# Input norm of an encoder block: scale and shift moved behind the transposes, and a new order of the first steps

## The chip, the cores and the metric

The kernel runs on one core of one Trainium2 chip. The metric is the device time of one execution in microseconds. Times of before are a median of three runs and one profiled execution of the same program.

## The reference, cut to what matters

The block has 512 tokens of 1024 features (D). What the change touches is the first norm and the first projection:

```python
mu = mean(x); var = mean((x - mu)**2)
u = (x - mu) * rsqrt(var + 1e-5) * ln_in_g + ln_in_b      # per token, g and b per feature
q, k, v, cb, cc, ch, ga, gb = split(u @ w_in)             # w_in: 1024 columns each for q, k, v and so on
mix = ...                                                 # attention, short convolution, gates
x = layer_norm(ALPHA * u + mix) ; x = layer_norm(ALPHA * x + moe(x))
```

So `u` is needed twice: transposed (features on partitions) as the operand of the projection, and as it is, by token, for the residual sum much later.

## The kernel before

Tokens lie in four tiles `u(0)` to `u(3)` of 128 rows, two to a page (`u_68`, `u_69` in the lists below). Every product with a weight is made of three float32r products: the activations are split into a high part (`uth`) and the rest (`utl`), and a weight unit of 256 columns into `hi_in` and `lo_in`. `Unit.split` makes these parts in two halves of four of the eight feature chunks each: ScalarE (ACT) casts `raw_in` to `hi_in`, and VectorE (DVE) or GpSimd (POOL) subtracts.

The order of the work is written out by hand: each engine takes its instructions in the order in which the Python code issues them. All loads named here go through SyncE's (SP's) queue, in code order too.

The start of the kernel has these steps:

- `bias_tile(h)`, four times: two products of TensorE (PE) and two copies by ACT, for the attention's relative bias.
- Per token tile: statistics (`norm_stats`, `norm_steps`: two BN_STATS, one BN_AGGR and a chain of nine small DVE instructions ending in `ln_rs`), then the norm. Tiles 0 and 1 take it on DVE as four instructions over 512 columns (`normalize`, L114 and L115), with `ln_in_g` and `ln_in_b` held as rows broadcast to 128 partitions (`gb_in`, 512 KB each). Tiles 2 and 3 take it in pieces on ACT, POOL and DVE (`normalize_apart`).
- `transpose_split`: eight PE transposes of a tile into two PSUM banks, then per bank one ACT cast to `uth` and one DVE subtraction to `utl`.
- `v_group(j, tt)`: 24 products of token tile tt with weight unit j (columns of v), then a DVE copy to `V`. There are 16 of them, written v00, v10, v01 and so on in this document (unit first, tile second). Three PSUM banks (`ps_mm`) hold their results.

After the sixteen v groups the projections by column follow (`col_group`, L509 to L511), and the rest of the block, which the change leaves as it is.

Pages are 22 buffers of 8 KB per partition; a load waits until the page that it takes is free.

Of the kernel before, what the change touches and what calls it, by code (L numbers as in the profile page):

```python
# [37 lines left out]
def block(ctx: ExitStack, tc, a, out, dump=None, stop=None):  # L38
# [228 lines left out]
    def transpose_split(src, dst_h, dst_l, tt):  # L267

        for i in range(2):
            ps = ps_tp.tile([128, 512], F32, name="tp")  # L270
            for k in range(4):
                nc.tensor.transpose(ps[:, k * 128:(k + 1) * 128],
                                    src[:, (i * 4 + k) * 128:(i * 4 + k + 1) * 128], ident)
            psv = ps.rearrange("p (k t) -> p k t", k=4)
            o = dst_h[i][:, :, tt * 128:(tt + 1) * 128]
            nc.scalar.copy(o, psv)
            nc.vector.tensor_sub(dst_l[i][:, :, tt * 128:(tt + 1) * 128], psv, o.bitcast(F32))
# [18 lines left out]
    def normalize_apart(t, mv, rs, g, b):  # L296

        nb = work.tile([128, 1], F32, name="ln_nb")
        nc.vector.scalar_tensor_tensor(nb, mv[:, 0:1], -1.0, rs, op0=OP.mult, op1=OP.mult)
        for h in HALF:  # L300
            nc.scalar.activation(t[:, h], t[:, h], AF.Identity, scale=rs, bias=nb)
            nc.gpsimd.tensor_mul(t[:, h], t[:, h], g[:, h])
        yield
        for h in HALF:
            nc.vector.tensor_add(t[:, h], t[:, h], b[:, h])

    moments = {}

    def input_steps(tt):
# [2 lines left out]
        moments[tt] = next(steps)
        yield
        yield from steps

    def apart(tt):
        return normalize_apart(u(tt), *moments[tt], g_in, b_in)
# [21 lines left out]
    together(input_steps(0))
    normalize(u(0), *moments[0], g_in, b_in)  # L340
    units[0].split(nc.gpsimd)
    transpose_split(u(0), UTH, UTL, 0)
# [1 line left out]
    chain = input_steps(1)
    next(chain)
    together(chain)
    normalize(u(1), *moments[1], g_in, b_in)
    units[1].split(nc.gpsimd, nc.gpsimd)
    state["split"] = 2
    v_group(0, 0)  # L350
    chain = input_steps(2)
    next(chain)
# [1 line left out]
    transpose_split(u(1), UTH, UTL, 1)
    together(chain)
    half = apart(2)
    next(half)
    together(input_steps(3))
    v_group(1, 0)
    together(half)  # L360
    half = apart(3)
    next(half)
    v_group(0, 1)
    v_group(1, 1)
    transpose_split(u(2), UTH, UTL, 2)
# [1 line left out]
    together(half)
    v_group(0, 2)
    transpose_split(u(3), UTH, UTL, 3)
    prm = setup[0:42, 1152:1280]  # L370
# [973 lines left out]
```

## Time and profile before

| | us |
|---|---|
| median of 3 runs | 1162.05 (1161.49 to 1163.46) |
| the profiled execution, its own time | 1163.4 |
| its span in the profile | 1161.7 |
| PE busy in the span | 1086.0 |
| DVE, ACT, POOL busy | 467.4, 274.9, 127.9 |

The span is cut by the first column group, whose first product starts at about 78.2 us. Everything that the change moves stands ahead of it, except the two loads of `gb_in` and the eight new DVE instructions that stand by the last v groups. The timeline is read per engine: start, duration, and in brackets how long the engine was idle before and what ended that. A row with xN holds N instructions that followed each other.

### The profile page before, as it was taken

How to read it: one execution, taken by the hardware profiler on the slowest of the kernel's cores; microseconds unless marked ns; L12 is line 12 of the kernel's file. 1: busy time of each engine (PE TensorE's matmuls, PEld its weight loads, DVE VectorE, ACT ScalarE, POOL GpSimd, SP SyncE). 2: the span in 40 equal slices, each digit the busy share in tenths (PEclk: the TensorE clock that was granted, in tenths of full speed). 3: DMA queues.
4: the chain of work that ended last, by engine and by line, in shares of the span. 5: the costliest groups of instructions: out<-in, count | busy, mean ns of one | idle time of the engine just before them, and what ended most of it. 6: DMA issues, size and time to landing. Idle time of an engine off the chain costs nothing.

```text
span 1161.7 us, 17381 instructions
## 1 busy us (share of the span) xinstructions
PE 1086.0 (93%) x7145; PEld 723.6 (62%) x7145; DVE 467.4 (40%) x1018; ACT 274.9 (24%) x491; POOL 127.9 (11%) x110
## 2 busy tenths in 40 slices
PE   5999999989999999999949998999999999999994
PEld 3998877767888888888945443545454544445442
DVE  6621565654244343147781123323223222322256
ACT  3403545743023323233221111111111111111002
POOL 2304322311000000023342000000000000000000
PEclk9999999999999999999968999999999999999997
DMA  8332212122332232434195899999999999999941
GB/s 302 106 118 72 74 37 73 52 84 82 109 103 79 73 106 75 145 113 141 40 395 199 318 409 359 411 394 410 399 408 408 395 409 401 409 407 356 409 165 74
DMA packets 103324, 264.86 MB, mean 228 GB/s; under 512 B 4528, under 2 KB 49644, under 8 KB 102732
## 3 DMA queue, kind: packets, MB, share of 16 engines
q1 hardware_dynamic: 102444, 262.53, 60.3%
q8 instruction: 59, 0.97, 0.3%
q10 hardware_dynamic: 576, 1.05, 0.2%
q0 software_dynamic: 224, 0.15, 0.2%
q14 instruction: 21, 0.17, 0.0%
HBM read 260.30 MB, written 3.41 MB: 227 GB/s over the span
## 4 chain that ended last, share of the span: by engine, by line
PE 84%; DVE 11%; DMA 1%; ACT 1%; issue 1%; POOL 1%; SPq 0%; ACTq 0%; DVEq 0%; POOLq 0%
PE gu L947 19%; PE mm L510 10%; PE mm L511 10%; PE mm L509 10%; PE y L974 10%; PE x L1005 5%; PE x L907 3%; PE x L908 3%; PE pv L460 2%; PE mm L287 2%; PE mm L289 2%; PE mm L288 2%; PE lg L434 1%; PE x L919 1%; DVE u L1007 1%
## 5 line engine op out<-in xcount | busy, mean ns | idle before, releaser
L509 PE MATMUL mm<-uth,hi_in 128*128 128x512 f32 x448 | 178.7, 399 | 0.0
L511 PE MATMUL mm<-uth,lo_in 128*128 128x512 f32 x448 | 174.5, 390 | 0.0
L510 PE MATMUL mm<-utl,hi_in 128*128 128x512 f32 x448 | 174.4, 389 | 0.0
L947 PE MATMUL gu<-wg,xg 128*32 128x512 f32 (+1 forms) x1024 | 133.4, 593 | 0.0
L947 PE MATMUL gu<-wu,xg 128*32 128x512 f32 (+1 forms) x1024 | 133.3, 592 | 0.0
L974 PE MATMUL y<-wd,ht 128*32 128x512 f32 (+1 forms) x1024 | 114.9, 601 | 0.7 <-ACT ht L966 0.7
L1007 DVE TENSOR_TENSOR u<-u,x 128x512 f32<-128x512 f32 x120 | 76.7, 684 | 52.1 <-PE x L1005 52.1
L510 PEld LDWEIGHTS mm<-utl,hi_in 128*128 128x128 f32 x448 | 84.2, 188 | 18.5 <-issue 1.0
L509 PEld LDWEIGHTS mm<-uth,hi_in 128*128 128x128 f32 x448 | 84.2, 188 | 18.4 <-issue 0.5
L511 PEld LDWEIGHTS mm<-uth,lo_in 128*128 128x128 f32 x448 | 84.1, 188 | 17.5
L957 DVE SCALAR_TENSOR_TENSOR h<-h,w,gu 128x512 f32<-128x512 f32 x16 | 12.0, 748 | 179.5 <-PE gu L947 179.5
L947 PEld LDWEIGHTS gu<-wu,xg 128*32 128x32 f32 x1024 | 33.3, 110 | 76.6 <-issue 73.0
L1005 PE MATMUL x<-ys,st 128*128 128x512 f32 x240 | 68.1, 405 | 12.5 <-DVE u L1007 7.1
L947 PEld LDWEIGHTS gu<-wg,xg 128*32 128x32 f32 x1024 | 32.9, 110 | 74.6 <-issue 70.9
L974 PEld LDWEIGHTS y<-wd,ht 128*32 128x32 f32 x1024 | 32.0, 111 | 72.4 <-issue 70.2
L169 POOL TENSOR_TENSOR lo_in<-raw_in,hi_in 128x1024 fp32r<-128x1024 f32 x25 | 59.1, 2384 | 146.3 <-ACT hi_in L168 95.7
L907 PE MATMUL x<-S,xh 128*128 128x256 f32 (+1 forms) x256 | 68.6, 301 | 0.6 <-POOL over L1030 0.6
L168 ACT CAST hi_in<-raw_in 128x1024 fp32r<-128x1024 f32 x64 | 63.6, 1045 | 14.9 <-DVE lo_wa L169 8.9
L908 PE MATMUL x<-S,xl 128*128 128x256 f32 (+1 forms) x256 | 66.1, 292 | 0.0
L169 DVE TENSOR_TENSOR lo_in<-raw_in,hi_in 128x1024 fp32r<-128x1024 f32 x39 | 46.0, 1220 | 46.1 <-ACT hi_in L168 45.9
L983 DVE TENSOR_TENSOR ys<-y,ys 128x512 fp32r<-128x512 f32 x30 | 20.6, 691 | 103.1 <-ACT ys L981 103.1
L1005 PEld LDWEIGHTS x<-ys,st 128*128 128x128 f32 x240 | 41.3, 188 | 25.0 <-DVE u L1007 13.1
(301 smaller groups left out, 1589.9 us busy)
## 6 DMA issues: line engine op xcount, KB each, us to landing
wg<-in_w_gate_e SPq DMA_DIRECT2D x64, 1024.0 KB, 12.5
wu<-in_w_up_e SPq DMA_DIRECT2D x64, 1024.0 KB, 12.9
wd<-in_w_down_e SPq DMA_DIRECT2D x64, 1024.0 KB, 9.3
raw_in<-in_w_in SPq DMA_DIRECT2D x32, 1024.0 KB, 5.6
raw_wa<-in_w_a_proj SPq DMA_DIRECT2D x4, 1024.0 KB, 5.1
raw_wb<-in_w_b_proj SPq DMA_DIRECT2D x4, 1024.0 KB, 5.1
raw_wo<-in_w_o SPq DMA_DIRECT2D x4, 1024.0 KB, 5.8
u<-in_x SPq DMA_DIRECT2D x4, 512.0 KB, 11.7
```

The costliest lines, as they stand in the source:

```text
L168: nc.scalar.copy(self.hi[:, k], self.raw[:, k])
L169: eng.tensor_sub(self.lo[:, k], self.raw[:, k], self.hi[:, k].bitcast(F32))
L287: nc.tensor.matmul(o, lh(k)[:, sl], unit.hi[:, k], start=(k == 0), stop=False)
L509: nc.tensor.matmul(ps, unit.hi[:, k, sl], xh(k), start=(k == 0), stop=False)
L510: nc.tensor.matmul(ps, unit.hi[:, k, sl], xl(k), start=False, stop=False)
L511: nc.tensor.matmul(ps, unit.lo[:, k, sl], xh(k), start=False, stop=(k == KC - 1))
L907: nc.tensor.matmul(o, part(XH, tt)[:, sl], r, start=(tt == 0), stop=False)
L908: nc.tensor.matmul(o, part(XL, tt)[:, sl], r, start=False, stop=(tt == NT - 1))
L947: nc.tensor.matmul(t[32 * p:32 * p + 32], disp[i // 2][:, k, base + 32 * p:base + 32 * p + 32], of_rows(w, sel, p), start=(k == 0), stop=( ...
L974: nc.tensor.matmul(Y[hf][32 * p:32 * p + 32], ht[:, f, 32 * p:32 * p + 32], of_rows(w, sel, p), start=(f == 0), stop=(f == 3))
L1005: nc.tensor.matmul(ps, l, r, start=(n == 0), stop=(n == len(terms) - 1))
L1007: nc.vector.tensor_add(o, o, ps)
```

## The change

The norm in front of the transposes now only subtracts the mean and multiplies by `ln_rs`. Tile 0 does it as one DVE instruction over 1024 columns (L315), tiles 1 to 3 as one ACT instruction (L319). Scale and shift come after the transposes, where a feature lies on a partition: `gcol` holds `ln_in_g` and `ln_in_b` as 16 columns (two small loads, one PE transpose, one ACT copy), and each 128-column piece of a transposed tile is copied from PSUM to a new SBUF tile `y_in` with its column of scale and shift: four pieces on DVE (first bank, L283) and four on ACT (second bank, L285). The cast to `uth` and the subtraction to `utl` then read `y_in`. The broadcast rows are loaded later, and `finish_input` applies them to `u` itself by two DVE instructions of 128x1024 per tile, behind the four groups v30 to v33.

The order of the steps changes as well; POOL no longer takes part in it. In the diff `together` runs its arguments in turns, a step each.

```diff
     nc.sync.dma_start(u(0), x_rows[0])
+    prm = setup[0:42, 1152:1280]
+    for i, n in enumerate(("ln_in_g", "ln_in_b")):
+        nc.sync.dma_start(prm[8 * i:8 * i + 8], a[n].rearrange("(k p) -> k p", p=128))
     nc.sync.dma_start(onehot, a["bucket_onehot"])
-    gb_in = page("gb_in", (128, 2, D))
-    for j, n in enumerate(("ln_in_g", "ln_in_b")):
-        nc.sync.dma_start(gb_in[:, j], a[n].rearrange("(o d) -> o d", o=1).to_broadcast([128, D]))
-    g_in, b_in = gb_in[:, 0], gb_in[:, 1]
...
-    def transpose_split(src, dst_h, dst_l, tt):
+    def turn_in(tt):
+        y = att.tile([128, KC, 128], F32, name="y_in", tag="p", bufs=3)
         for i in range(2):
             ps = ps_tp.tile([128, 512], F32, name="tp")
...
+            for j in range(4):
+                k = 4 * i + j
+                g, b, p = gcol[:, k:k + 1], gcol[:, 8 + k:9 + k], ps[:, j * 128:(j + 1) * 128]
+                if i == 0:
+                    nc.vector.tensor_scalar(y[:, k], p, g, b, op0=OP.mult, op1=OP.add)
+                else:
+                    nc.scalar.activation(y[:, k], p, AF.Identity, scale=g, bias=b)
+            o = UTH[i][:, :, tt * 128:(tt + 1) * 128]
+            part = y[:, 4 * i:4 * i + 4]
+            nc.scalar.copy(o, part)
+            nc.vector.tensor_sub(UTL[i][:, :, tt * 128:(tt + 1) * 128], part, o.bitcast(F32))
+            yield
...
+    def input_norm(tt, eng):
+        steps = norm_steps(norm_stats(u(tt)))
+        mv, rs = next(steps)
+        together(steps)
+        if eng is nc.vector:
+            nc.vector.tensor_scalar(u(tt), u(tt), mv[:, 0:1], rs, op0=OP.subtract, op1=OP.mult)
+        else:
+            nb = work.tile([128, 1], F32, name="ln_nb")
+            nc.vector.scalar_tensor_tensor(nb, mv[:, 0:1], -1.0, rs, op0=OP.mult, op1=OP.mult)
+            nc.scalar.activation(u(tt), u(tt), AF.Identity, scale=rs, bias=nb)
...
     bias_tile(0)
+    input_norm(0, nc.vector)
+    together(turn_in(0), units[0].split_steps())
+    input_norm(1, nc.scalar)
+    units[1].split()
+    v_group(0, 0)
+    together(turn_in(1))
     bias_tile(1)
+    input_norm(2, nc.scalar)
+    v_group(0, 1)
+    v_group(1, 0)
+    together(turn_in(2))
+    v_group(1, 1)
     bias_tile(2)
+    input_norm(3, nc.scalar)
+    v_group(0, 2)
+    together(turn_in(3))
+    units[2].split()
+    state["split"] = 3
     bias_tile(3)
+    v_group(2, 0)
+    gb_in = page("gb_in", (128, 2, D))
...
+    def finish_input(tt):
+        nc.vector.tensor_mul(u(tt), u(tt), gb_in[:, 0])
+        nc.vector.tensor_add(u(tt), u(tt), gb_in[:, 1])
...
-        v_group(2, tt)
+        if tt:
+            v_group(2, tt)
...
         v_group(3, tt)
+        finish_input(tt)
```

The groups on PE stood in the order v00, v10, v01, v11, v02, v12, v03, v13, v20 to v33; now they stand as v00, v01, v10, v11, v02, v20, v12, v03, v13, v21 to v33. (The loop of the third unit, which held v20, now begins with v21.)

Three places show it in the engines' own order. On DVE, from the end of tile 1's chain (`ln_rs`) on, before:

```order
L85 TENSOR_TENSOR ln_rs<-ln_i,ln_t 128x1
L114 SCALAR_TENSOR_TENSOR u_68<-u_68,ln_mv,gb_in 128x512
L115 SCALAR_TENSOR_TENSOR u_68<-u_68,ln_rs,gb_in 128x512
L114 SCALAR_TENSOR_TENSOR u_68<-u_68,ln_mv,gb_in 128x512
L115 SCALAR_TENSOR_TENSOR u_68<-u_68,ln_rs,gb_in 128x512
L294 COPY v_117<-mm 128x256
L100 BN_STATS ln_st<-u_69 128x6 x2
L107 BN_AGGR ln_mv<-ln_st 128x2
L277 TENSOR_TENSOR utl_115<-tp,uth_113 128x4x128
L277 TENSOR_TENSOR utl_116<-tp,uth_114 128x4x128
```

And the same place now (`lo_in_200` is the rest of weight unit 1, `v_116` the copy of v00):

```order
L85 TENSOR_TENSOR ln_rs<-ln_i,ln_t 128x1
L318 SCALAR_TENSOR_TENSOR ln_nb<-ln_mv,ln_rs 128x1
L168 TENSOR_TENSOR lo_in_200<-raw_in_106,hi_in_199 128x1024 x2
L307 COPY v_116<-mm 128x256
L283 TENSOR_SCALAR y_in<-tp,gcol 128x128 x4
L289 TENSOR_TENSOR utl_114<-y_in,uth_112 128x4x128
L289 TENSOR_TENSOR utl_115<-y_in,uth_113 128x4x128
L100 BN_STATS ln_st<-u_69 128x6 x2
L107 BN_AGGR ln_mv<-ln_st 128x2
```

The two subtractions of weight unit 1 came from POOL to DVE and stand between tile 1's norm and its copies. Tile 2's statistics stand behind tile 1's last subtraction, and no longer in front of both.

On ACT, the first instructions behind the copies of the first bias tile, before (`hi_in_149` is unit 0, `hi_in_197` unit 1):

```order
L168 CAST hi_in_149<-raw_in_104 128x1024 x2
L276 CAST uth_113<-tp 128x4x128
L276 CAST uth_114<-tp 128x4x128
L329 COPY bias_119<-lg 128x512
L329 COPY bias_119<-lg 128x128
L168 CAST hi_in_197<-raw_in_107 128x1024 x2
```

And now (`hi_in_161` is unit 0, `hi_in_199` unit 1):

```order
L288 CAST uth_112<-y_in 128x4x128
L167 CAST hi_in_161<-raw_in_103 128x1024
L285 ACTIVATE y_in<-tp,gcol 128x128 x4
L288 CAST uth_113<-y_in 128x4x128
L167 CAST hi_in_161<-raw_in_103 128x1024
L319 ACTIVATE u_68<-u_68,ln_nb,ln_rs 128x1024
L167 CAST hi_in_199<-raw_in_106 128x1024 x2
L288 CAST uth_112<-y_in 128x4x128
L285 ACTIVATE y_in<-tp,gcol 128x128 x4
L288 CAST uth_113<-y_in 128x4x128
```

The casts of the weights now alternate with the tile's; tile 1's norm stands on ACT, in front of unit 1's casts.

On DVE, from `ln_rs` of tile 3 on, now (`lo_in_459` is the rest of unit 2; the copy behind it is that of v20):

```order
L85 TENSOR_TENSOR ln_rs<-ln_i,ln_t 128x1
L318 SCALAR_TENSOR_TENSOR ln_nb<-ln_mv,ln_rs 128x1
L307 COPY v_117<-mm 128x256
L283 TENSOR_SCALAR y_in<-tp,gcol 128x128 x4
L289 TENSOR_TENSOR utl_114<-y_in,uth_112 128x4x128
L289 TENSOR_TENSOR utl_115<-y_in,uth_113 128x4x128
L168 TENSOR_TENSOR lo_in_459<-raw_in_109,hi_in_458 128x1024 x2
L307 COPY v_116<-mm 128x256
```

Before, the same stretch read so (`lo_in_457` is the rest of unit 2; the copies behind it are those of v12 and v03):

```order
L299 SCALAR_TENSOR_TENSOR ln_nb<-ln_mv,ln_rs 128x1
L294 COPY v_117<-mm 128x256 x2
L277 TENSOR_TENSOR utl_115<-tp,uth_113 128x4x128
L277 TENSOR_TENSOR utl_116<-tp,uth_114 128x4x128
L305 TENSOR_TENSOR u_69<-u_69,gb_in 128x512 x2
L294 COPY v_118<-mm 128x256
L277 TENSOR_TENSOR utl_115<-tp,uth_113 128x4x128
L277 TENSOR_TENSOR utl_116<-tp,uth_114 128x4x128
L169 TENSOR_TENSOR lo_in_457<-raw_in_110,hi_in_456 128x1024 x2
L294 COPY v_118<-mm 128x256 x2
```

Before, tile 3's statistics were done ahead of tile 2's copies, and unit 2's parts stood in front of the copies of v12 and v03, which don't need them. Now tile 3's norm ends ahead of only its own copies, and the next group on PE is one of unit 2.

## Rows read from the trace of the kernel before

**Rows 1.** The page's part 4: chain that ended last, by engine.

```profile
PE 84%; DVE 11%; DMA 1%; ACT 1%; issue 1%; POOL 1%; SPq 0%; ACTq 0%; DVEq 0%; POOLq 0%
```

**Rows 2.** PE's waits, 0 to 80 us: who, for whom, total us, times, longest.

```profile
PE tp L272 <- issue: 7.2, 2, 3.8
...
PE mm L288 <- DVE utl L277: 0.3, 1, 0.3
```

**Rows 3.** Timeline of PE: start, us, line, count, and idle time before in brackets.

```profile
11.90 1.08 PE L272 MATMUL tp<-ident,u 128*128 128x128 f32 x4 [3.81 <-issue]
...
16.78 0.58 PE L287 MATMUL mm<-hi_in,uth 128*128 128x256 f32 x1
...
21.83 1.34 PE L328 MATMUL lg<-setup 32*128 32x512 f32 x4
26.52 1.09 PE L272 MATMUL tp<-ident,u 128*128 128x128 f32 x4 [3.34 <-issue]
...
28.75 0.56 PE L287 MATMUL mm<-hi_in,uth 128*128 128x256 f32 x1
29.11 0.42 PE L288 MATMUL mm<-hi_in,utl 128*128 128x256 f32 x1
...
38.70 1.04 PE L272 MATMUL tp<-ident,u 128*128 128x128 f32 x8
...
54.19 0.25 PE L405 MATMUL tp<-ident,setup 42*128 42x42 f32 x1
...
55.06 0.39 PE L287 MATMUL mm<-hi_in,uth 128*128 128x256 f32 x1
```

**Rows 4.** Timeline of DVE, a v group's copy; tile `mm`, 68 to 100 us.

```profile
64.00 0.42 DVE L294 COPY v<-mm 128x256 f32<-128x256 f32 x1 [2.46 <-PE mm L289]
...
L509 PE MATMUL mm<-uth,hi_in x33: 388/389/397, 78.2 to 100.0; 128*128 128x512 f32 x33
```

**Rows 5.** Timeline of DVE, tile 0's norm and tile 1's chain.

```profile
5.24 1.29 DVE L100 BATCH_NORM_STATS2 ln_st<-u 128x6 f32<-128x512 f32 x2 [5.24 <-DMA u<-in_x]
...
8.52 0.16 DVE L85 TENSOR_TENSOR ln_rs<-ln_i,ln_t 128x1 f32<-128x1 f32 x1
...
11.05 0.75 DVE L115 SCALAR_TENSOR_TENSOR u<-u,ln_rs,gb_in 128x512 f32<-128x512 f32 x1 [0.66 <-DMA gb_in<-in_ln_in_b]
...
19.40 2.18 DVE L77 SCALAR_TENSOR_TENSOR ln_t<-ln_i,ln_v 128x1 f32<-128x1 f32 x1
21.61 2.27 DVE L79 SCALAR_TENSOR_TENSOR ln_i<-ln_t,ln_i 128x1 f32<-128x1 f32 x1
```

**Rows 6.** Timeline of ACT: unit 0's first casts, tile 2's norm.

```profile
13.76 1.99 ACT L168 CAST hi_in<-raw_in 128x1024 fp32r<-128x1024 f32 x2 [5.30 <-DMA raw_in<-in_w_in]
...
32.80 1.52 ACT L301 ACTIVATE u<-u,ln_nb,ln_rs 128x512 f32<-128x512 f32 x2 [3.08 <-DVE ln_nb L299]
```

**Rows 7.** Lines by form, DVE and ACT: busy us, mean ns of one, idle before.

```profile
L1007 DVE TENSOR_TENSOR u<-u,x 128x512 f32<-128x512 f32 x120 | 76.7, 684 | 52.1 <-PE x L1005 52.1
L169 DVE TENSOR_TENSOR lo_in<-raw_in,hi_in 128x1024 fp32r<-128x1024 f32 x39 | 46.0, 1220 | 46.1 <-ACT hi_in L168 45.9
...
L100 DVE BATCH_NORM_STATS2 ln_st<-u 128x6 f32<-128x512 f32 x16 | 10.1, 673 | 5.2 <-DMA u<-in_x 5.2
...
L467 DVE TENSOR_SCALAR o<-pv,sm 128x256 f32<-128x256 f32 x16 | 8.7, 543 | 0.6
...
L625 ACT CAST czh<-conv 128x512 fp32r<-128x512 f32 x8 | 5.0, 622 | 30.5 <-DVE conv L624 30.5
...
L301 ACT ACTIVATE u<-u,ln_nb,ln_rs 128x512 f32<-128x512 f32 x4 | 3.0, 808 | 7.7 <-DVE ln_nb L299 7.7
...
L329 ACT COPY bias<-lg 128x128 f32<-128x128 f32 x4 | 1.1, 278 | 0.0
```

**Rows 8.** Windows: us, busy of PE, PEld, DVE, ACT, POOL, granted clock, DMA.

```profile
24.70:31.40 6.70, 4.47 (x20) 4.13 (x21) 6.46 (x16) 1.17 (x2) 0.00 (x0) 0.50 1.01 332
31.50:48.00 16.50, 16.15 (x127) 15.11 (x127) 12.52 (x32) 7.42 (x12) 10.66 (x11) 1.00 0.28 61
```

More of the change, by code (lines that the diff above doesn't have):

```diff
@@ L162, in load, with split_steps @@
             nc.sync.dma_start(self.raw, self.src)
-        def split(self, eng=nc.vector, first=nc.vector):
+        def split_steps(self, eng=nc.vector, first=nc.vector):
             self.hi = page("hi_" + self.name, (128, KC, 256), F32R)
@@ L169, in split @@
                 eng.tensor_sub(self.lo[:, k], self.raw[:, k], self.hi[:, k].bitcast(F32))
+                yield
+        def split(self, eng=nc.vector, first=nc.vector):
+            together(self.split_steps(eng, first))
     def win_unit(col):
@@ L265, in block @@
     utl = lambda k: UTL[k // 4][:, k % 4, :]
-    def transpose_split(src, dst_h, dst_l, tt):
+    def turn_in(tt):
+        y = att.tile([128, KC, 128], F32, name="y_in", tag="p", bufs=3)
         for i in range(2):
             ps = ps_tp.tile([128, 512], F32, name="tp")
[L271 to L277, printed above, removed]
+            for j in range(4):
+                k = 4 * i + j
+                nc.tensor.transpose(ps[:, j * 128:(j + 1) * 128], u(tt)[:, k * 128:(k + 1) * 128], ident)
+            for j in range(4):
+                k = 4 * i + j
+                g, b, p = gcol[:, k:k + 1], gcol[:, 8 + k:9 + k], ps[:, j * 128:(j + 1) * 128]
[7 more added lines that the diff above has]
+            nc.vector.tensor_sub(UTL[i][:, :, tt * 128:(tt + 1) * 128], part, o.bitcast(F32))
+            yield
     V = [page(f"v{i}", (128, 2, D)) for i in range(2)]
@@ L294, in v_group @@
                   lambda o: nc.vector.tensor_copy(V[tt // 2][:, tt % 2, j * 256:(j + 1) * 256], o))
[L296 to L309, printed above, removed]
-        steps = norm_steps(norm_stats(u(tt)))
[L312 to L317, printed above, removed]
+    def input_norm(tt, eng):
+        steps = norm_steps(norm_stats(u(tt)))
+        mv, rs = next(steps)
[6 more added lines that the diff above has]
+            nc.scalar.activation(u(tt), u(tt), AF.Identity, scale=rs, bias=nb)
     biases = [page(f"bias{i}", (128, 2, 1024)) for i in range(2)]
@@ L336, in skew_bias @@
         nc.gpsimd.memset(BT[0:64, h, 448:512], NEG)
+    gcol = early.tile([128, 16], F32, name="gcol")
+    ps = ps_tp.tile([128, 512], F32, name="tp")
+    nc.tensor.transpose(ps[:, 0:16], prm[0:16], ident[0:16, 0:16])
+    nc.scalar.copy(gcol, ps[:, 0:16])
     bias_tile(0)
[L339 to L342, printed above, removed]
-    bias_tile(1)
[L344 to L352, printed above, removed]
-    bias_tile(2)
[L354 to L365, printed above, removed]
-    bias_tile(3)
[L367 to L370, printed above, removed]
+    input_norm(0, nc.vector)
[4 more added lines that the diff above has]
+    together(turn_in(1))
+    bias_tile(1)
+    input_norm(2, nc.scalar)
[3 more added lines that the diff above has]
+    v_group(1, 1)
+    bias_tile(2)
+    input_norm(3, nc.scalar)
[3 more added lines that the diff above has]
+    state["split"] = 3
+    bias_tile(3)
+    v_group(2, 0)
+    gb_in = page("gb_in", (128, 2, D))
+    for j, n in enumerate(("ln_in_g", "ln_in_b")):
+        nc.sync.dma_start(gb_in[:, j], a[n].rearrange("(o d) -> o d", o=1).to_broadcast([128, D]))
+    def finish_input(tt):
+        nc.vector.tensor_mul(u(tt), u(tt), gb_in[:, 0])
+        nc.vector.tensor_add(u(tt), u(tt), gb_in[:, 1])
     lqk = setup[0:1, 1280:1792].rearrange("p (a m d) -> p a m d", a=2, m=2)
```

## The prediction

> **What bounds the kernel now.** I read the chain of waits first: 84% of the span lies on PE [rows 1]. So the change is worth what it takes from, or adds to, PE's path before the first column group, at 78.2 us [rows 4]; what follows is the same work in the same order, and a shift there goes through to the end. Next I read PE's waits and timeline up to there. PE waits 7.2 us ahead of two sets of transposes (3.8 us ahead of tile 0's, 3.3 us ahead of tile 1's) [rows 2, 3]. From the first product of v10 at 28.75 on it runs almost without a gap; the one wait worth naming is 0.3 us for tile 2's `utl` [rows 2, 3]. [...]
>
> So before, once tile 1 is through, every later tile's norm and parts are hidden behind v groups of 2.88 us each (a copy of 0.42 after 2.46 of waiting for PE) [rows 4]. The question is whether that still holds with the new order.
>
> **Prices.** DVE: 128x512 with two tensors 0.68, 128x1024 1.22, so 1.05 ns a column [rows 7]. The new copy on DVE (128x128 from PSUM, two pointers) has no row; the nearest is L467, the same operation with two pointers from PSUM at 256 columns, 0.54 [rows 7]. Less 128 columns: 0.41. Following instructions overlap by 0.06 (a pair of BN_STATS takes 1.29, not 2 x 0.673) [rows 5, 7], so four take 3 x 0.34 + 0.41 = 1.43. On ACT: a 128x128 copy from PSUM takes 0.278, and two pointers add 0.808 - 0.622 = 0.19 [rows 7], so 0.46; with 0.10 of overlap (two L301 in 1.52) [rows 6] four take 3 x 0.36 + 0.46 = 1.54. Bounds: 0.28 each (the plain copy on ACT), 1.2 for four; 0.54 each without overlap (L467 itself), 2.2 for four. I take 1.43 and 1.54, from the nearest rows. The cast from SBUF is 0.62 (L625), the rest of half a unit 1.22 [rows 7], the cast of half a unit 1.0 (two in 1.99) [rows 6]. ACT's norm over 1024 columns: 0.81 (L301) and 0.43 for 512 columns more, which is what a half cast of 1024 takes beyond the 0.62 of 512: 1.24. DVE's norm of tile 0 has no row: 0.68 (half the columns) to 1.50 (two L115); I take 1.22, the two-tensor instruction of that shape [rows 5, 7]. It moves tile 0 by less than 0.6 us either way.
>
> [...]
>
> **What is removed.** Tile 0's norm no longer waits for the broadcast rows: `ln_rs` is there at 8.68, and L115 still waited for its row at 11.05 [rows 5]. Unit 0's load has 1 MB less ahead of it, so its casts need not wait until 13.76 [rows 6]. POOL is idle at the start, so the 2.18 and 2.27 us that two instructions of 0.2 us took in tile 1's chain go [rows 5]: 4.1 us.
>
> **The new path, tile by tile** (us; hand-overs 0.05).
> *Tile 0.* Norm 8.68 to 9.90; transposes at half clock (1.08 for four) 9.95 to 12.1; copies on DVE 11.1 to 12.55; cast 13.2. Then ACT: unit 0's first half 14.2, four copies 15.75, cast 16.35, second half 17.35. DVE follows: 13.95, 15.45, 17.05, 18.6. v00 gets its third product at 15.45 and its second half at 18.6, and ends at about 20.9. Before, the bias product behind it starts at 21.83 [rows 3]: 0.9 won.
> *Tile 1.* DVE is free for it only at 18.6. Its statistics and chain take 3.44 (5.24 to 8.68) [rows 5] and 0.17 for `ln_nb`: 22.2. ACT norm 23.5, unit 1's casts 25.5, rests on DVE 26.9, the copy of v00 27.25, tile 1's four copies 28.7, cast 29.35, `utl` 30.05. PE transposes at 23.5, does a bias tile until 28.2 and waits; v01's second product comes at 30.1. Before, the second product of the group in that place stood at 29.11 with three bias tiles done [rows 3]; now two are. That is 1.0 + 1.34 = 2.3 behind. The 4.1 us won on DVE pay for unit 1's rests (2.4, now on DVE) and the longer turn.
> *Tile 2.* Its turn is hidden: v01 and v10 end at about 36.9 (before, three groups took from 28.75 to 38.70, 1.3 of it clock [rows 3]), and u(2) is ready at 37.1 (`utl` of tile 1 32.25, chain 35.85, norm).
> *Tile 3.* The cycle from transposes to transposes: first four 0.55, DVE 1.43, cast 0.62, ACT 1.54, cast 0.62, `utl` 0.68, copy of v11 0.34, chain and `ln_nb` 3.6, norm 1.24 and hand-overs of 0.2: 10.8 us, from 37.1 to 47.9. PE has only 1.0 + 2.88 + 1.34 + 2.88 = 8.1 us to do: idle from 45.2 to 47.9, 2.7 us.
> *Unit 2.* Behind tile 3's transposes (half clock, to 50.1) and a bias tile (to 52.6) PE comes to v20, which needs unit 2's parts, and these stand behind tile 3's turn: copies 50.5, cast 51.1, ACT 52.65, cast 53.3, unit 2's cast 54.3, rest 55.55. PE waits 1.8 us for the cast and 1.0 more for the rest, though v12, behind it, has its operands. v20 then runs at half clock (0.21 a product instead of 0.12) to about 60.3.
> *The sum.* From there ten groups (28.8) and the small products between v13 and the next group (54.19 to 55.06, 0.9) [rows 3] end at 90.0, against 78.2: **11.8 us later**. In other words: 2.3 behind after tile 1, 0.2 at u(2), 2.7 at u(3), 2.8 at unit 2, and some 4 by the clock (transposes and a bias tile 1.2 each, v20 2.0), less a little that before lost in small waits.
>
> **What I cost at nothing.** `finish_input`: eight instructions of 1.22, 9.8 us on DVE beside v30 to v33. With the copy (0.34) it is 2.8 per group of 2.88, plus unit 4's rests; DVE falls some 2 us behind, which three banks cover, and unit 4's rests stand ahead of three of the four. Without that cover: 2 to 3 us. The two broadcast loads now stand ahead of the small parameters and of unit 3's load on SP, which has some 40 us until use. The bias round trips wait for unit 2's page until about 55.6; attention needs them long after. `gcol` is off the path unless its loads come after 8 us: its transpose and bias tile 0 fit before 9.9.
>
> **Rivals.**
> *It is faster.* Before, POOL's blocking, the loads and the gap ahead of tile 1 are real (4.1, 2.4, 3.3), and if a tile's turn fits into PE's 8.1 us, PE runs through from v00: 20.9 + 15 x 2.88 + 3 x 1.0 + 3 x 1.34 + 0.9 + 1.3 clock = 73.3, 4.9 us earlier, 1157.2. It decides at a cycle of 8.1 instead of 10.8. Even at 0.28 a piece the cycle is 10.1. Chance 0.05.
> *The same.* PE waits only ahead of v01 (2.3) and the rest is hidden, because tile 3's chain or unit 2's parts come earlier than I have them: 1164. Chance 0.06.
> *The clock stays up in the 2.7 us gap.* The trace shows a fall in a gap of 3.3 and none in 0.3 [rows 2, 3, 8]; 2.7 lies nearer the first. If it stays, tile 3's transposes take 1.0 instead of 2.2 and part of v20 is fast: about +9, 1171. Chance 0.25; it is of the forecast's sign.
>
> **How the numbers follow.** The sum is against the profiled execution: 1163.4 + 11.8 = 1175.2; the median lies 1.35 below that execution, so 1162.05 + 11.8 = 1173.9. The likeliest case is that, chance 0.64: four copies at 1.2 give about +9 and four at 2.2 (the chain then longer by 1.5 for each of the last two tiles) about +15. The range takes in the clock case and most of both bounds: 1167.5 to 1178. 0.2% is 2.3 us, about what a measurement here tells from no change: slower 0.89, same 0.06, faster 0.05.
>
> **What would show it.** In the changed profile: tile 1's `ln_rs` near 22 and none of its small instructions over 0.5 us; PE's waits led by its transposes of `u` for ACT's L319 and by the first products of v01 and v20 for DVE's L289 and L168 (each 1 to 3 us); the first column group near 90; granted clock 0.50 for a second time around 48 to 60. I am wrong if the pieces on DVE and ACT take 0.2 us or less, if PE shows no wait behind 40 us, or if v20 starts before 50.

## The result, and the profile after

The changed kernel takes 1172.71 us (median of four runs, 1170.87 to 1175.09) against 1161.88 us of the kernel before on the same chip (1161.49 to 1163.46): a ratio of 1.009, 95% interval 1.0078 to 1.0103. It is slower by some 10.8 us; the prediction was 1173.9, in a range of 1167.5 to 1178. The span of the profiled execution went from 1161.7 to 1172.0 us, 10.3 more. The last steps of lines L272, L287 to L289, L328 and L509 to L511 of before are L278, L300 to L302, L330 and L512 to L514 now.

The tile `mm` after, 60 to 110 us (instructions, least, median and longest ns, first and last start): the first column group stands at 88.4, where [rows 4] have 78.2. So 10.2 of the 10.3 us were lost ahead of it, and nothing behind it changed the sum.

```profile
L512 PE MATMUL mm<-uth,hi_in x32: 389/389/396, 88.4 to 109.5; 128*128 128x512 f32 x32
```

The chain that ended last, by engine, answers [rows 1]: PE went from 84% to 83%.

```profile
PE 83%; DVE 11%; ACT 2%; issue 2%; POOL 1%; DMA 0%; ACTq 0%; SPq 0%; DVEq 0%; POOLq 0%
```

PE's waits after, 0 to 100 us (us in all, times, longest), answer [rows 2]:

```profile
PE tp L278 <- ACT u L319: 5.7, 2, 3.3
PE mm L300 <- ACT hi_in L167: 5.6, 2, 3.3
PE tp L342 <- DMA setup<-in_ln_in_b: 5.3, 1, 5.3
PE tp L278 <- DVE u L315: 1.3, 1, 1.3
PE mm L300 <- ACT uth L288: 1.2, 1, 1.2
PE mm L302 <- DVE lo_in L168: 0.9, 2, 0.5
```

The 5.3 us are the first wait of the program, for `gcol`'s load, ahead of tile 0 and off the path. All others but the 1.3 stand behind tile 0's transposes: 13.4 us. Where they stand, PE's timeline tells, in answer to [rows 3]:

```profile
9.20 1.97 PE L278 MATMUL tp<-ident,u 128*128 128x128 f32 x8 [1.30 <-DVE u L315]
13.45 0.58 PE L300 MATMUL mm<-hi_in,uth 128*128 128x256 f32 x1 [2.29 <-ACT hi_in L167]
...
22.53 1.97 PE L278 MATMUL tp<-ident,u 128*128 128x128 f32 x8 [3.33 <-ACT u L319]
24.43 2.50 PE L330 MATMUL lg<-setup 32*128 32x512 f32 x4
28.12 0.58 PE L300 MATMUL mm<-hi_in,uth 128*128 128x256 f32 x1 [1.19 <-ACT uth L288]
...
35.73 1.09 PE L278 MATMUL tp<-ident,u 128*128 128x128 f32 x8
...
46.44 1.09 PE L278 MATMUL tp<-ident,u 128*128 128x128 f32 x8 [2.41 <-ACT u L319]
47.46 1.46 PE L330 MATMUL lg<-setup 32*128 32x512 f32 x4
52.20 0.58 PE L300 MATMUL mm<-hi_in,uth 128*128 128x256 f32 x1 [3.28 <-ACT hi_in L167]
53.46 0.58 PE L302 MATMUL mm<-lo_in,uth 128*128 128x256 f32 x1 [0.47 <-DVE lo_in L168]
```

Tile 0's transposes stand 2.7 us earlier than before (11.90). Behind them PE waits ahead of tile 1's transposes, as before (3.33 us, before 3.34), and in four places where before it ran without a gap: 2.29 + 0.47 us in v00, 1.19 us ahead of v01, 2.41 us ahead of tile 3's transposes and 3.28 + 0.47 us in v20. The prices of the new instructions, lines by form in answer to [rows 7] (busy us, mean ns of one):

```profile
L285 ACT ACTIVATE y_in<-tp,gcol 128x128 f32<-128x128 f32 x16 | 6.0, 453 | 0.0
L283 DVE TENSOR_SCALAR y_in<-tp,gcol 128x128 f32<-128x128 f32 x16 | 5.5, 404 | 3.0 <-PE tp L278 3.0
L319 ACT ACTIVATE u<-u,ln_nb,ln_rs 128x1024 f32<-128x1024 f32 x3 | 3.7, 1241 | 12.1 <-DVE ln_nb L318 12.1
L315 DVE TENSOR_SCALAR u<-u,ln_mv,ln_rs 128x1024 f32<-128x1024 f32 x1 | 0.8, 812 | 0.0
```

And windows of after, in answer to [rows 8] (us, then busy time of PE, PEld, DVE, ACT and POOL, granted clock, DMA): between 49 and 56 us the granted clock is at 0.50 a second time (as from 22.5 to 31 us), first with PE standing still and then under v20. The first line shows the start of the program.

```profile
10.00:20.00 10.00, 6.38 (x30) 5.19 (x28) 7.34 (x16) 4.53 (x8) 0.00 (x0) 1.00 1.08 278
...
36.00:44.00 8.00, 8.00 (x60) 7.08 (x58) 5.67 (x16) 3.40 (x8) 0.00 (x0) 1.00 0.05 19
44.00:49.00 5.00, 2.51 (x13) 1.54 (x12) 2.63 (x11) 1.71 (x2) 0.00 (x0) 0.95 0.00 0
49.00:52.00 3.00, 0.00 (x0) 0.00 (x0) 1.38 (x2) 2.97 (x7) 0.00 (x0) 0.50 0.00 0
52.00:56.00 4.00, 3.33 (x14) 3.04 (x15) 2.36 (x2) 1.75 (x4) 0.00 (x0) 0.50 0.10 28
```

PE's time up to the first column group splits into four parts that add up: when tile 0's transposes start; the waits behind them; the work, which at the full rate is 55.0 us in each kernel (16 groups of 2.88, four sets of transposes of 1.0, three bias tiles of 1.34, 0.9 of small products); and what that work took above this, called the excess below. From the profiles of before, of after and of seven experiments (the two with added products, e6 and e8, are left out of this table):

| kernel | tile 0's transposes | waits behind | excess | first column group | time (median) |
|---|---|---|---|---|---|
| before | 11.9 | 4.4 | 6.9 | 78.2 | 1161.9 |
| after | 9.2 | 13.4 | 10.8 | 88.4 | 1172.7 |
| e3, after without copies by column | 9.2 | 5.9 | 9.6 | 79.7 | 1163.4 |
| e4, new norm and copies in the old order | 9.3 | 8.3 | 8.6 | 81.2 | 1165.1 |
| e1, v20 moved back | 9.65 | 9.45 | 13.3 | 87.4 | 1170.9 |
| e2, tile 3's norm moved forward | 9.7 | 12.1 | 12.6 | 89.4 | 1175.1 |
| e5, e1 and e2 together | 10.1 | 8.7 | 10.4 | 84.2 | 1166.1 |
| e7, a third order | 9.4 | 2.4 | 7.0 | 73.8 | 1155.0 |
| e9, e7 without copies by column | 9.5 | 2.1 | 6.6 | 73.2 | 1153.5 |

After less before: start -2.7, waits +9.0, excess +3.9, in all +10.2. The table needs three remarks.

- The excess is put down to the clock. Where the granted clock is 0.50 that is what the rows say. But tile 0's transposes and v00 are as slow (3.4 us of after's excess, products 0.21 us apart up to 17.97) while the granted clock reads 1.00, as the window from 10 to 20 us shows. That the clock is behind this part too is read from the spacing of the products and not shown.
- After, e1, e2 and e5 begin with the same steps, but tile 0's transposes start between 9.2 and 10.1 us, as the load of `u(0)` ends sooner or later (DVE's first BN_STATS at 4.85 in after, 5.72 in e5). A difference of under 1 us between two rows may be no more than that.
- All columns but the last come from one profiled execution of each kernel. From the first column group to the end of the span it is 1079.6 us (e9) to 1084.3 us (e2), though PE has the same work there in all of them, so more than 4 us of a difference in time can arise behind the column group. One place is the attention's output projection: 42.9 us from its first product to its last in e5 (272.1 to 315.0), 44.6 us in after (276.2 to 320.8), with a granted clock in the first 4 us of 1.00 and 0.66. What the moved steps are worth is therefore read at the column group.

### The profile page after: what moved, and what is told of

Its sections match the earlier page's. It is cut to its first block, busy times and chain, and to the rows that moved or that the text cites. A ratio compares the mean times of both kernels' runs of the same rounds, so it can differ in the third digit from the quotient of the medians.

```text
span 1172.0 us, 17404 instructions
## 1 busy us (share of the span) xinstructions
PE 1089.9 (93%) x7146; PEld 725.9 (62%) x7146; DVE 473.7 (40%) x1035; ACT 281.9 (24%) x507; POOL 116.1 (10%) x103
## 4 chain that ended last, share of the span: by engine, by line
PE 83%; DVE 11%; ACT 2%; issue 2%; POOL 1%; DMA 0%; ACTq 0%; SPq 0%; DVEq 0%; POOLq 0%
PE gu L952 19%; PE mm L513 10%; PE mm L512 10%; PE mm L514 10%; PE y L979 10%; PE x L1010 5%; PE x L912 3%; PE x L913 3%; PE mm L302 2%; PE mm L300 2%; PE mm L301 2%; PE pv L463 2%; PE lg L437 1%; PE x L924 1%; DVE u L1012 1%
## 5 line engine op out<-in xcount | busy, mean ns | idle before, releaser
L512 PE MATMUL mm<-uth,hi_in 128*128 128x512 f32 x448 | 178.6, 399 | 0.0
L514 PE MATMUL mm<-uth,lo_in 128*128 128x512 f32 x448 | 174.6, 390 | 0.0
L512 PEld LDWEIGHTS mm<-uth,hi_in 128*128 128x128 f32 x448 | 84.1, 188 | 18.4 <-issue 0.5
L514 PEld LDWEIGHTS mm<-uth,lo_in 128*128 128x128 f32 x448 | 84.1, 188 | 17.8
L168 DVE TENSOR_TENSOR lo_in<-raw_in,hi_in 128x1024 fp32r<-128x1024 f32 x42 | 49.6, 1221 | 47.6 <-ACT hi_in L167 47.6
L167 ACT CAST hi_in<-raw_in 128x1024 fp32r<-128x1024 f32 x64 | 63.7, 1045 | 8.9 <-DVE lo_wa L168 8.9
L168 POOL TENSOR_TENSOR lo_in<-raw_in,hi_in 128x1024 fp32r<-128x1024 f32 x22 | 51.9, 2381 | 134.8 <-ACT hi_in L167 84.4
## 6 DMA issues: line engine op xcount, KB each, us to landing
wd<-in_w_down_e SPq DMA_DIRECT2D x64, 1024.0 KB, 10.8
```

What stands on the lines that cost most here:

```text
L512: nc.tensor.matmul(ps, unit.hi[:, k, sl], xh(k), start=(k == 0), stop=False)
L514: nc.tensor.matmul(ps, unit.lo[:, k, sl], xh(k), start=False, stop=(k == KC - 1))
```

## The experiments

The theory behind the prediction: the copies by column lengthen each tile's turn on DVE and ACT, and the new order leaves PE no group to do meanwhile; so PE waits, and the clock falls in the waits. Rivals: the copies cost their length wherever they stand; the order alone costs it; the clock alone. "Column group at" below gives the start of the first column group, in us; a ratio is that to the kernel before, with its 95% interval.

### Which part of the change: e3 and e4

**e3** keeps the new order and drops the copies; the casts read PSUM as before (scale and shift are left out of the projection's operand).

```diff
-        y = att.tile([128, KC, 128], F32, name="y_in", tag="p", bufs=3)
...
-            for j in range(4):
-                k = 4 * i + j
-                g, b, p = gcol[:, k:k + 1], gcol[:, 8 + k:9 + k], ps[:, j * 128:(j + 1) * 128]
-                if i == 0:
-                    nc.vector.tensor_scalar(y[:, k], p, g, b, op0=OP.mult, op1=OP.add)
-                else:
-                    nc.scalar.activation(y[:, k], p, AF.Identity, scale=g, bias=b)
...
-            part = y[:, 4 * i:4 * i + 4]
+            part = ps.rearrange("p (k t) -> p k t", k=4)
```

> The changed kernel without the copies by column: the cast and the subtraction read PSUM, and scale and shift are left out of the projection's operand (this part of the computation is missing). It takes four DVE copies (1.37 us) and four ACT copies (1.50 us) out of each tile's turn and leaves the order as it is. Theory A: the cycle from transposes to transposes shrinks from 10.7 to about 7.5 us, under PE's 8.1, so the wait for u(3) shrinks to about 1, that for unit 2's parts to about 1.3; tile 1's turn comes about 4 us earlier; first column group 77 to 80.5, time 1162 to 1165. If only the order counted whatever the turn's length: above 1168.

Measured: 1163.44 us, ratio 1.0007 (0.9995 to 1.0018); column group at 79.7. As expected. PE's waits in e3, 0 to 100 us: where after has 13.4 us behind tile 0's transposes, 5.9 are left, and the longest takes 2.5 us instead of 3.3. Behind them, the line of the tile `mm` with the column group's start.

```profile
PE tp L277 <- ACT u L311: 3.5, 2, 2.5
PE mm L294 <- DVE lo_in L168: 1.2, 2, 0.8
PE mm L292 <- ACT hi_in L167: 1.2, 2, 0.8
```

```profile
L504 PE MATMUL mm<-uth,hi_in x44: 389/389/477, 79.7 to 109.4; 128*128 128x512 f32 x44
```

**e4** does the opposite: the new norm and the copies in the order of before.

```diff
-    together(turn_in(0), units[0].split_steps())
-    input_norm(1, nc.scalar)
-    units[1].split()
+    units[0].split(nc.gpsimd)
+    together(turn_in(0))
+    bias_tile(1)
+    input_norm(1, nc.vector)
+    units[1].split(nc.gpsimd, nc.gpsimd)
     v_group(0, 0)
+    bias_tile(2)
     together(turn_in(1))
-    bias_tile(1)
     input_norm(2, nc.scalar)
+    input_norm(3, nc.scalar)
+    v_group(1, 0)
     v_group(0, 1)
-    v_group(1, 0)
+    v_group(1, 1)
     together(turn_in(2))
-    v_group(1, 1)
-    bias_tile(2)
-    input_norm(3, nc.scalar)
+    bias_tile(3)
     v_group(0, 2)
     together(turn_in(3))
-    units[2].split()
-    state["split"] = 3
-    bias_tile(3)
-    v_group(2, 0)
+    state["split"] = 2
...
-        if tt:
-            v_group(2, tt)
+        v_group(2, tt)
```

> The new norm and the copies by column in the order of steps of the kernel before (unit 0's second half and unit 1's parts on POOL again, three bias tiles early, v10 ahead of v01, v12 and v03 ahead of unit 2; the broadcast rows loaded late and applied behind v30 to v33, as in the change). Theory A: the longer turns are mostly hidden; one wait of about 3 us for tile 2's turn ahead of v02 is paid by the start without the rows; first column group 77 to 79, time 1160 to 1163, the same as before within 0.2%. Rival C: each of four tiles pays 1.4 to 2.9 us for its copies on PE's path: 1167 or more.

Measured: 1165.05 us, ratio 1.0032 (1.002 to 1.0044); column group at 81.2. Missed by some 2 us, and as far from the rival's 1167. The expectation left out that POOL still does unit 1's rests there, and holds up tile 1's chain on DVE as it did before [rows 5]; what e4 would take without that hold was not run. DVE's timeline of e4, and behind it POOL's: two instructions of 0.2 us take 1.49 and 2.27, until 24.25, where POOL's two are through (19.56 + 4.68).

```profile
20.27 0.15 DVE L74 TENSOR_SCALAR ln_i<-ln_v 128x1 int32<-128x1 int32 x1
20.46 1.49 DVE L77 SCALAR_TENSOR_TENSOR ln_t<-ln_i,ln_v 128x1 f32<-128x1 f32 x1
21.98 2.27 DVE L79 SCALAR_TENSOR_TENSOR ln_i<-ln_t,ln_i 128x1 f32<-128x1 f32 x1
24.29 0.22 DVE L77 SCALAR_TENSOR_TENSOR ln_t<-ln_i,ln_v 128x1 f32<-128x1 f32 x1
```

```profile
19.56 4.68 POOL L168 TENSOR_TENSOR lo_in<-raw_in,hi_in 128x1024 fp32r<-128x1024 f32 x2 [3.45 <-ACT hi_in L167]
```

What follows from the two: the new norm and copies in the old order cost 3.0 us at the column group (the hold by POOL included), the new order without its copies 1.5, both 10.2. The remaining 5.7 belong to neither alone. That speaks against "the copies cost their length" and against "the order costs it".

### The two new waits: e1, e2 and e5

**e1** moves v20 back behind v13, so that PE does not come to it before unit 2's parts stand:

```diff
     bias_tile(3)
-    v_group(2, 0)
...
-        if tt:
-            v_group(2, tt)
+        v_group(2, tt)
```

**e2** puts tile 3's statistics and norm in front of tile 2's copies:

```diff
     v_group(1, 0)
+    input_norm(3, nc.scalar)
     together(turn_in(2))
     v_group(1, 1)
     bias_tile(2)
-    input_norm(3, nc.scalar)
```

**e5** makes both edits.

> The changed kernel with one group moved: v20 stands behind v13 again, as before the change, so that v12 follows the last bias tile. Theory A (the line of work on DVE and ACT is too long for the group that PE takes next): v12 has its operands when the bias tile ends (48.9 us in the changed kernel's profile), so the waits of 3.28 and 0.47 us ahead of and in v20 go, and most of its 3 us of half clock; first column group at 81.5 to 83.5 instead of 88.4; time 1166 to 1168 (changed kernel 1172.7). Rival C (the copies by column cost PE time wherever the groups stand): PE waits as long in another place; 1171 to 1173.

> The changed kernel with tile 3's statistics and norm moved in front of tile 2's copies (where before the change they stood, too). Theory A: u(3) is ready near 39, so PE's wait of 2.41 us ahead of tile 3's transposes goes; tile 2's copies come 1.5 us later, which v11 and the bias tile cover but for some 0.3; v20 still waits for unit 2's parts. First column group near 86.5 to 88; time 1170 to 1172. Rival C: the same wait comes back at tile 2's turn, no gain.

Measured: e1 1170.88 us, ratio 1.0069 (1.0042 to 1.0097), column group at 87.4; e2 1175.05 us, ratio 1.0112 (1.0092 to 1.0131), column group at 89.4. Both miss what was expected, and neither is clear of the changed kernel (1.0078 to 1.0103). In e1 the waits in v20 are gone (9.45 us in all, not 13.4), so the rival, that PE waits as long in another place, falls, though the time is close to the rival's 1171. But the excess rose by 2.5. Of this 1.85 stand at tile 3's transposes and the bias tile behind them: the wait ahead is as long as in after, 2.40 us, but in after the two took 2.48 us together (46.44 to 48.92) and in e1, at the low clock (0.71 on average from 46 to 50 us, 0.50 from 50 to 55), 4.33 (47.74 to 52.07). Earlier, v00, v01 and v10 ran slow for longer (products 0.21 us apart up to 20.25 in v00, in after up to 17.97; a granted clock of 0.60 from 30 to 35 us, in after 0.85), and tile 2's transposes start at 37.09 though ACT had `u(2)` ready at 36.12. PE's timeline and a window of e1:

```profile
47.74 1.97 PE L278 MATMUL tp<-ident,u 128*128 128x128 f32 x8 [2.40 <-ACT u L319]
49.64 2.50 PE L330 MATMUL lg<-setup 32*128 32x512 f32 x4
```

```profile
50.00:55.00 5.00, 5.00 (x17) 3.73 (x17) 2.70 (x4) 4.67 (x9) 0.00 (x0) 0.50 0.00 0
```

Its four runs lie 5.8 us apart (1166.79 to 1172.64), so part of them may have gone the other way; the one trace is of the slowest. In e2 the wait for `u(3)` went, but the rival was right that there is no gain: waits of 0.98 + 0.29 us came up at v02 (tile 2's turn is longer by the norm put in front), v02 took 4.84 us at a granted clock of 0.64 (42.6 to 47.4 us), where it took 3.14 in after, and v20's waits stayed, 3.40 + 0.47. Each move alone leaves a wait that is followed by the low clock.

> The two moves of e1 and e2 together: v20 behind v13 again, and tile 3's statistics and norm in front of tile 2's copies. Mine (a wait goes only when PE has another group whose operands stand ready; each move alone left the other wait, together they leave none): the waits ahead of tile 3's transposes and ahead of v20 both go, the rest stay as in e1 and e2: 2.3 ahead of v00, 0.5 at its rests, 3.0 ahead of tile 1's transposes, 1.2 ahead of v01's second product, 1.0 and 0.3 at v02. Sum 8.3 us, no wait behind v02. First column group at 82 to 84.5, time 1166 to 1168, as fast as e1 or up to 4 us faster. Rival (the clock gives back what the waits bring, as e1's excess of 13.3 us over full rate against 10.8 in the changed kernel suggests): waits go as said but the column group stays at 86 or later, time 1170 or more.

Measured: 1166.11 us, ratio 1.004 (1.0025 to 1.0055), column group at 84.2; waits 8.7 us, none behind v02. Met, on time as on waits. Two moves that take no work away bring the column group 4.2 us forward. The median falls by 6.6 us and the profiled span by 6.9, but 2.7 of these lie behind the column group, where the moves change nothing of PE's work (1.7 in the output projection, see the remarks on the table). So a good part of the loss hangs on which work stands ready for PE while a tile is turned, as the theory has it.

### The clock by itself: e6 and e8

e6 and e8 are the changed kernel with products added whose results nothing reads, in places where PE waits, to keep the clock up. The edit of e6:

```diff
+    fill_ps = ps_pv.tile([128, 2, 256], F32, name="pv")
+
+    def fill(n):
+        for _ in range(n):
+            nc.tensor.matmul(fill_ps[:, 0], uth(0)[:, 0:128], units[0].hi[:, 0], start=True, stop=True)
...
     v_group(0, 0)
+    fill(15)
     together(turn_in(1))
     bias_tile(1)
+    fill(5)
...
+    fill(20)
     together(turn_in(3))
...
     bias_tile(3)
+    fill(27)
     v_group(2, 0)
```

And of e8 against e6:

```diff
     bias_tile(1)
-    fill(5)
+    fill(24)
...
     v_group(1, 0)
+    fill(12)
     together(turn_in(2))
```

> The changed kernel, with products added whose results nothing reads (unit 0's first product of a group, 128x256 into a bank that is free until attention): 15 ahead of tile 1's transposes, 5 behind bias tile 1, 20 ahead of tile 3's transposes, 27 ahead of v20, that is about as many as fit into PE's waits there. What has to be done otherwise, and what waits for what, is the same. Theory 1 (of the changed kernel's loss, waits of 9.0 us and a clock at its lower level for 3.9 us more are two different terms, and the second follows from PE standing still): the granted clock stays at 1.00 from v00 on, tile 1's transposes take about 1.0 instead of 1.97, bias tile 1 1.34 instead of 2.50, v20's products 0.12 instead of 0.21; since the chains on DVE and ACT are as before, only v20 and what follows starts from the same place and runs faster: first column group at 83 to 85.5, time 1167 to 1170. Theory 2 (the waits alone count, or the clock falls here for another reason than PE's stand): v20 at 0.21 a product again, column group at 88 or later, time 1172 or more.

> The changed kernel with more of the products whose results nothing reads: 15 ahead of tile 1's transposes, 24 (not 5) behind bias tile 1, 12 ahead of tile 2's transposes, 20 ahead of tile 3's, 27 ahead of v20. With 5 behind bias tile 1 PE stood still for 2.4 us ahead of v01, and the clock was low until 34.4; v20 at full rate took 2.3 us less, but started 1.5 us later than in the changed kernel. Theory 1 (the chains on DVE and ACT set when tiles 2 and 3 and unit 2 are ready, whatever PE's clock is; the clock adds only what v20 loses, 2.3 us): v01 and v10 at 0.12 a product, tile 2's transposes at 35.5 to 36.3, tile 3's at 46.2 to 47.2, v20's first product at 51.8 to 53, first column group at 85.6 to 87, time 1169 to 1171.5. Theory 2 (the 3.9 us that PE lost to the clock are all to be had, on top of the waits): column group at 84.5 or earlier, time 1168 or less.

Measured: e6 1171.23 us, ratio 1.0087 (1.0069 to 1.0105), column group at 87.6; e8 1172.2 us, ratio 1.0077 (1.0062 to 1.0092), column group at 87.4. Neither time is clear of the changed kernel's (1.0078 to 1.0103). The clock under v20 did what was expected (in e6 v01 and v10 still ran slow, at 0.50 from 28 to 32 us and 0.68 from 32 to 36), the time did not: e6 lies between its two theories, and e8 above the first and far from the second. PE's timeline of e8, then a window of it:

```profile
37.16 1.03 PE L278 MATMUL tp<-ident,u 128*128 128x128 f32 x8
...
47.81 1.09 PE L278 MATMUL tp<-ident,u 128*128 128x128 f32 x8
48.83 1.34 PE L330 MATMUL lg<-setup 32*128 32x512 f32 x4
50.10 3.49 PE L344 MATMUL pv<-hi_in,uth 128*128 128x256 f32 x27
53.58 0.38 PE L300 MATMUL mm<-hi_in,uth 128*128 128x256 f32 x1
54.84 0.38 PE L302 MATMUL mm<-lo_in,uth 128*128 128x256 f32 x1 [0.76 <-DVE lo_in L168]
```

```profile
52.00:56.00 4.00, 3.24 (x25) 2.85 (x24) 2.98 (x3) 3.24 (x6) 0.00 (x0) 1.00 0.00 0
```

From tile 2's transposes to tile 3's it is 10.65 us in e8 (37.16 to 47.81) and 10.71 in after (35.73 to 46.44); from there to v20's first product 5.77 and 5.76. In e8 PE was busy all through these stretches and in after it stood still for 5.7 us of them, at a clock that fell to 0.50; the length is the same, so DVE's and ACT's chain sets it. From v20's first product to the column group e8 takes 33.85 us (53.58 to 87.43) and after 36.18 (52.20 to 88.38), 2.3 less. But tile 2's transposes stood 1.4 us later in e8: 0.5 because its tile 0 started 0.5 later (9.72, not 9.20), and 0.9 because the added products ran past `u(2)`, a cost of the added products themselves. So of 88.4 us 2.3 came off and 1.4 came on, which gives 87.4 with the decimals kept. My expectations had the right sign and overrated the size, in e6 most, since they let v20 start no later than before.

What the two show: of the 3.9 us of excess in the sum above, only the 2.3 from v20 on lie on the path. Slow products ahead of a wait use up the wait: in after v01 and v10 took 7.61 us instead of 5.76, but ended just as ACT had `u(2)` ready, at 35.67. They cost what they take beyond that, 1.0 us in e1 (37.09 against 36.12).

### A third order: e7 and e9

**e7** keeps the new norm and the copies and writes a third order. Tile 1's norm stands on DVE in front of the weights' rests; two of these go to POOL; two bias tiles stand where PE would wait; and groups stand between the turns, and within tile 2's. The lines that stand there now (helpers and lines taken out are left out):

```diff
+    input_stats(0)
+    input_norm(0, V_)
+    next(turns[0])
+    input_stats(1)
+    units[0].half(0, P_)
+    input_norm(1, V_)
+    bias_tile(1)
+    units[1].half(0, V_)
+    units[1].half(1, V_)
+    next(turns[0])
+    bias_tile(2)
+    units[0].half(1, V_)
+    input_stats(2)
+    next(turns[1])
+    next(turns[1])
+    units[2].half(1, P_)
+    input_norm(2, S_)
+    v_group(0, 0)
+    v_group(1, 0)
+    bias_tile(3)
+    input_stats(3)
+    v_group(0, 1)
+    units[2].half(0, V_)
+    next(turns[2])
+    input_norm(3, V_)
+    v_group(1, 1)
+    next(turns[2])
+    v_group(2, 0)
+    next(turns[3])
+    next(turns[3])
...
     v_group(1, 2)
+    v_group(0, 2)
     v_group(0, 3)
```

> The new norm and the copies by column in a third order, aimed at both kernels: tile 1's statistics and norm (on DVE) in front of unit 0's rests; unit 0's first rest and unit 2's second on POOL; tile 2 normed on ACT, tile 3 on DVE in front of the second half of tile 2's turn; bias tiles 1 and 2 behind tile 1's transposes as work for PE while its parts are made; groups v00, v10, v01, v11, v20, then v12, v02, v03, v13 with the heads' preparation. Mine (the copies cost only where PE has no group to do in the meantime): PE waits ahead of v00 and at tile 2's transposes, under 6 us in all behind tile 0's transposes, first column group at 71 to 76, time 1154 to 1160, faster than the kernel before by 2 to 7 us. Rival (an instruction of POOL with two tensors holds up the small instructions of the norm on DVE, as in the kernel before, 2.2 us each; or unit 1's load comes late): waits of over 8 us, column group at 77 to 81, time 1161 to 1165.

Measured: 1154.96 us (1151.72 to 1156.34), ratio 0.9935 (0.9919 to 0.995): faster than both kernels, 6.6 us below before and some 17.8 below the changed kernel. Column group at 73.8, as expected. PE's waits of e7, 0 to 100 us, its timeline, and the line with the column group's start:

```profile
PE tp L285 <- DVE u L328: 2.8, 3, 1.6
...
PE tp L285 <- ACT y_in L292: 0.3, 1, 0.3
```

```profile
14.14 2.50 PE L343 MATMUL lg<-setup 32*128 32x512 f32 x4
18.23 1.12 PE L285 MATMUL tp<-ident,u 128*128 128x128 f32 x4 [1.60 <-DVE u L328]
19.61 1.11 PE L285 MATMUL tp<-ident,u 128*128 128x128 f32 x4 [0.27 <-ACT y_in L292]
20.38 0.56 PE L307 MATMUL mm<-hi_in,uth 128*128 128x256 f32 x1
```

```profile
L541 PE MATMUL mm<-uth,hi_in x52: 389/389/580, 73.8 to 109.8; 128*128 128x512 f32 x52
```

v00 starts only at 20.38, 6.9 us later than in after, and from there PE waits only 0.49 us, ahead of tile 3's transposes. The span lies 7.3 us below that of before, 4.4 of it ahead of the first column group. Of the other 2.9, a wait ahead of the attention's output transposes that fell from 2.4 to 0.5 us is one part, and the output projection behind it, 43.0 us instead of 44.6, another; why that wait fell is open.

**e9** is e7 without the copies by column, cut as in e3 (scale and shift are left out of the projection's operand).

> The third order without the copies by column: the casts and the rests read the transposes from PSUM; the input norm's scale and shift are left out of the projection's operand. In the changed kernel's order leaving the copies out took 8.7 us off the first column group and 9.3 us off the time. Mine (the copies cost what PE stands still for, and in the third order it has other work nearly everywhere; only the wait ahead of tile 1's transposes, 1.6 us, and small ones, 1.2 us in all, hang on them): column group 71.5 to 74 against 73.8, time 1152 to 1155 against 1155.0. Rival (the copies cost their length on DVE and ACT in any order): column group at 68 or earlier, time 1149 or less.

Measured: 1153.46 us (1152.36 to 1154.78), ratio 0.9919 (0.9906 to 0.9933), column group at 73.2:

```profile
L533 PE MATMUL mm<-uth,hi_in x448: 387/389/796, 73.2 to 477.3; 128*128 128x512 f32 x150
```

As the theory has it: the copies that cost 8.7 us at the column group in the changed order (88.4 and 79.7) cost 0.6 in this one. The rival, that they cost their length on DVE and ACT in any order, falls. One limit: the third order was written with the copies in mind. In e9 the wait ahead of the first four of tile 1's transposes shrinks from 1.60 to 0.40 us, but one of 1.69 us, for DVE, comes up ahead of the other four. An order written for the kernel without copies was not run, and could be faster than e9.

## Why the prediction was right, point by point

**Prices.** Four copies on DVE 1.43, measured 1.37; four on ACT 1.54, measured 1.50 (a piece 0.404 and 0.453, where the prediction has 0.41 and 0.46); cast 0.62, measured 0.618; ACT's norm 1.24, measured 1.241. The working by the nearest rows held. Tile 0's norm was taken at 1.22 and is 0.81.

**Removed.** Tile 1's chain has no instruction over 0.22 us behind its two BN_STATS, and its `ln_rs` is there at 21.0, so the 4.1 us of POOL's hold did go (POOL has no instruction from 9.77 to 57.53 us). Tile 0's transposes stand at 9.20 (9.95 predicted), unit 0's first cast at 12.36 (13.2), and v00's third product at 14.71 (15.45).

**Tile 1: right in kind, too large.** `u(1)` at 22.5 (23.5 predicted); v01's second product at 28.85 (30.1). With one bias tile fewer done than before that is 28.85 - 29.11 + 1.34 = 1.1 us behind, where the sum has 2.3. Most of it is the start: tile 0 came 0.75 earlier.

**Tile 2.** 0.2 predicted, none measured.

**Tile 3: confirmed.** Cycle of 10.8 predicted, 10.71 measured; wait 2.7, measured 2.41.

**Unit 2: right in kind, too small.** 1.8 + 1.0 predicted, 3.28 + 0.47 measured. The parts came 5.8 us behind tile 3's transposes, not 6.4 as predicted, but PE was through with the bias tile 2.5 us behind them and not 4.7, and so waited longer; that is the next point. The prediction's list of signs had these first products wait for DVE's L289 and L168; they wait mostly for ACT, v01's for the cast of the tile (L288, 1.19) and v20's for the cast of the weights (L167, 3.28).

**The clock: the term that failed.** I had tile 3's transposes and bias tile 3 at half rate, a loss of 2.4 us; they took 1.09 and 1.46, a loss of 0.2. The half rate was an estimate, from the one gap of 3.34 us in [rows 3] and the 0.50 behind it in [rows 8]; no run shows that it follows every gap, and behind the 2.41 us of after the granted clock was 1.00 from 46.4 to 47.5 us and 0.50 from 49 to 56. The rival "the clock stays up in the gap" was right there, and wrong for v20, which I had at 2.0 of loss and which lost 2.4 (5.65 us without its waits, against 3.23 in e8). e1 shows how little a trace can say ahead on this: there a gap of 2.40 us ahead of the same transposes was followed by the low clock (0.50 from 50 to 55 us). And e8 shows that I should have asked of each slow stretch whether a wait follows it: up to the length of that wait it costs nothing. Tile 3's slow transposes would by this have cost little, since v20's wait of 3.28 us stood behind them and would have been shorter.

The terms together: 1.1 + 0 + 2.4 + 3.75 + 2.4 and 0.2 for the transposes and the bias tile is 9.9 of 10.2 us, where the sum had 11.8. The two terms that were too large, at tile 1 and at the clock, were in part made up by unit 2's, which was too small. The waits that the prediction named are the ones that came; that the total lies within 2 us is in part luck, since the clock ahead of v20 was wrong.

**Costed at nothing.** `finish_input` took 1.22 an instruction as predicted, and DVE was busy for 9.9 of the 10 us from 80 on; the first column group does not wait for it. The late bias round trips and the moved loads show in none of PE's waits.

**Rivals.** That it is faster hung on a cycle of 8.1 us; it is 10.71. But e7 shows the condition to be too narrow: a cycle may be longer than the work between two turns, if another group's operands stand ready. I had taken the order as given, and under the given order the condition holds. The rival "the same", that PE waits only ahead of v01, falls with the 2.41 us ahead of tile 3's transposes and the 3.75 in v20.

## What to carry to other kernels

In this kernel the instructions added to the side engines had no price of their own: the same copies cost 8.7 us in the changed order, 3.0 together with the new norm in the old order, and 0.6 in the third, by whether the engine that bounds the kernel had other work whose operands stood ready. So compute the cycle of the side engines from one turn to the next, and set beside it, in code order, the work that the bound engine can do meanwhile; where it falls short, try moving groups before you shorten instructions, and look at the next wait too, since one removed alone may come back as another wait or as slow products (e1, e2). Count slow products only as far as they outlast the wait that follows them. And check in the profile how much of a gain stands where the change is: here more than 4 us of a difference could stand elsewhere.
